# A transformer block on one core: first chunk of x on another DMA queue, the bias product one step later, seven warm-up products instead of nine

## The chip, the cores and the metric

The kernel runs on one core of a Trainium2 chip. The metric is the device time of one execution in microseconds (us). Before the change it is 303.93 us, the median of 3 runs (303.37 to 304.09). A run whose engines were recorded took 304.98 us, and its trace is what this document reads.

## The reference, cut to what matters

A single block on x of 256 tokens by 1024 columns, in float32. The part that stands at the start of the kernel is the input projection, and beside it a bias by distance for the attention's logits:

```
u    = rms_norm(x, mix_norm_g)              # x / rms(x) * g, row by row
proj = u @ w_in                             # 1024 -> 3*512 (q, k, v) + 2*512 (glu_a, glu_g)
attn = attention(q, k, v) with rel_bias[bucket(distance)] added to the logits, causal
conv = silu(layer_norm(depthwise_conv31(glu_a * sigmoid(glu_g))))
h    = x + concat(attn, conv) @ w_out
h    = h + (silu(un @ w_gate) * (un @ w_up)) @ w_down,   un = rms_norm(h, ffn_norm_g)
out  = rms_norm(h, final_norm_g)
```

## The kernel before, in words

All large products are made from float32 data split into two parts: a high part `wh` (or `uh`) and the rest `wl` (or `ul`), so each product is three: high by high, high by rest, rest by high. ScalarE (or VectorE for the first two pieces) makes the high part of a weight, and VectorE subtracts it for the rest. So every piece of a weight goes through a transfer (`raw_...`), a cast (`wh_...`) and a subtraction (`wl_...`) before TensorE has all three.

x lies transposed in `xs`, as 8 chunks (`k` = 0 to 7) of 128 columns by 256 tokens. `upper_u` (ScalarE) makes `uh[k]` from `xs[k]` and the gain in `pv`; `lower_u` (VectorE) makes `ul[k]`. The division by the root mean square of each token is not done there: it is applied to the products later, through `rb`, which comes from the sum of squares `accx`.

The first projection is worked in two halves. Step `a0.k` (function `a0`) does all for one chunk of the first half: cast, `uh`, `ul`, subtraction, and 12 matmuls of 128x256 into the banks `pa` and `pg` (`a_mm`). Steps `a1.i` do two chunks each of the second half with weights `a1_0` and `a1_1`. Between the steps of `a1` stand the sum of squares (`sq.k`, a square on ScalarE and an addition to `accx` on VectorE) and `rs` (`scale_x`), whose first instructions are TensorE's four small products `ps_x` with `accx`.

The order of all this is written out by hand, in the string `PROGRAM`: each word is a step, and every engine runs its own instructions in the order in which the steps issue them. `pz` (`bias_mm`) is the product of the table of the bias, `rbt`, with a constant one-hot matrix, `hot_s`; `zs` copies it out of the bank on ScalarE, `zd` sends it to memory from GpSimd's queue, and `bd` reads it back into `bias`, which `t.0` needs about 40 us into the run.

Transfers: SyncE's queue issues the pieces of the weights and the chunks of x in turn (lines 186 to 188). Of SyncE's and ScalarE's transfers at most eight are under way; a ninth waits for the landing of the one eight places before it. ScalarE's queue issues the first 28 columns of `pv`, which hold the gains (line 183). GpSimd's queue issues `hot_s` and `rbt` (lines 190 and 191), and after its fills the rest of `pv` (line 205). While the first data are on the way, TensorE runs `WARM` products of a matrix of ones with itself into a bank that nobody reads (line 194), which are there for its clock alone.

Of the kernel before, what the change touches and what calls it, by code (L numbers as in the profile page):

```python
# [16 lines left out]
S = 256  # L17
# [4 lines left out]
NB = 32  # L22
# [13 lines left out]
LOOK = 2  # L36
FINE = ("a0_0", "a0_4")
COPY_V = (("a0_0", 0), ("a0_0", 1))
WARM = 9

PROGRAM = """
ld.a1_0 a0.0 pz a0.1 a0.2 a0.3 zs zd ld.a1_1 a0.4 a0.5 a0.6 a0.7 ld.qk0
w.a1_0.0 sq.0 sq.1 w.a1_0.1 sq.2 sq.3 sq.4 ld.qk1 bd a1.0 w.a1_1.0 sq.5 sq.6 sq.7 h.a1_1.1 h.qk0.0 h.qk0.1 a1.1 rs
w.a1_1.1 w.qk0.0 ld.qk2 a1.2 rb glu.0 ud.0 w.qk0.1 ld.v0 us.0 a1.3 w.qk1.0 w.qk1.1 glu.1 ud.1 us.1 ld.qk3
qk.0.0 qk.0.1 qo.0 cw.0 h.qk2.0 h.qk2.1 qk.1.0 sc.0 qk.1.1 w.qk2.0 t.0 w.qk2.1 ct.0.0.1 ld.v1 qo.1 c.0.0 h.v0.0 n.0 ct.0.1.3 sc.1 t.1 h.v0.1 ct.0.3.4 w.v0.0
# [14 lines left out]
def block_kernel(ctx, tc, xT, w_in, w_out, w_gate, w_up, w_down, pvec, gfin, relb, hot, out):  # L60
# [10 lines left out]
    def mm(*args, **kw):  # L71
        return tc.keep_in_program_order(nc.tensor.matmul(*args, **kw))  # L72
# [12 lines left out]
    act, vec, pool, sync = (InOrder(e) for e in (nc.scalar, nc.vector, nc.gpsimd, nc.sync))  # L85

    def bank(i, name):
        return psum.tile([P, 512], F32, tag=f"b{i}", name=name)
# [78 lines left out]
    xs = const.tile([P, KD, S], F32, name="xs")  # L167
# [8 lines left out]
    rbt = w1.tile([NB + 1, H], F32, name="rbt")  # L176
    hot_s = w1.tile([NB + 1, ZN], F32, name="hot_s", tag="lg", bufs=2)
# [2 lines left out]
    wstk = [w1.tile([P, 8 * Q, 32], F32, name=f"wstk{i}", tag="wstk", bufs=2) for i in range(2)]  # L180
    invc = w1.tile([P, P], F32, name="invc")
    vec.memset(warm, 0.0)
    act.dma_start(pv[:, 0:PV_T], pvec[:, 0:PV_T])
    act.activation(warm, warm, AF.Sigmoid)
    first = [load(w_in, 2048 * i, f"a0_{4 * i}") for i in range(2)]
    for k in range(KD):
        next(first[k // 4])
        sync.dma_start(xs[:, k], xT[:, k * S : (k + 1) * S])
    pool.memset(ones, 1.0)
    pool.dma_start(hot_s, hot)  # L190
    pool.dma_start(rbt[0:NB, :], relb)
    wm = bank(4, "wm")
    for i in range(WARM):
        mm(wm[:, 0:P], ones, ones, start=i == 0, stop=i == WARM - 1)
    pool.memset(ident, 0.0)
    pool.affine_select(out=ident, in_=ident, compare_op=ALU.not_equal, fill=1.0, base=0,
                       pattern=[[-1, P]], channel_multiplier=1)
    pool.memset(mhalf, -0.5)
    pool.memset(rbt[NB : NB + 1, :], 1.0)
    for t in upad:  # L200
        pool.memset(t[:, 0 : TAPS - 1], 0.0)
        pool.memset(t[:, TAPS - 1 + S : UW + TAPS - 1], 0.0)
        pool.memset(t[:, UW + TAPS - 1 + S :], 0.0)
# [140 lines left out]
    zs = w1.tile([H, ZN], F32, name="zs", tag="lg", bufs=2)  # L344
    zd = dram.tile([H, ZN], F32, name="zd")
# [275 lines left out]
    for g in range(FG):  # L621
# [4 lines left out]
        if g == 0:  # L626
            act, vec, pool, sync = nc.scalar, nc.vector, nc.gpsimd, nc.sync
# [130 lines left out]
```

## Time and profile before

| | |
|---|---|
| median of the runs | 303.93 us (303.37 to 304.09) |
| the profiled execution | 304.98 us |
| its span, from the first to the last recorded instruction | 303.2 us |
| TensorE busy | 294.6 us, 97% of the span |
| VectorE, ScalarE, GpSimd busy | 72%, 55%, 3% |
| moved by the DMA engines | 56.39 MB, mean 186 GB/s over the span |

Reading it: the times in the trace are counted from the start of the span. PE is TensorE's matmul, DVE VectorE, ACT ScalarE, POOL GpSimd, SP SyncE; a q behind a name (SPq) is the part of the engine that issues transfers. A number in brackets behind a row is how long the engine had stood idle before it, and what released it. A float32 product shows as two matmul records, so the nine warm-up products are 18 records. All helpers that record an instruction have the line 72, 75 or 83, and the names in the rows tell them apart: `u` is `uh` and `ul`, and `raw_a`, `wh_a` and `wl_a` are the weights of both halves of the first projection.

### The profile page before, as it was taken

Reading aid. Unit: us, or ns where it says so; the run is one execution under the profiler, and the core shown is the slowest. Engines: PE = TensorE matmul, PEld = TensorE weight load, DVE = VectorE, ACT = ScalarE, POOL = GpSimd, SP = SyncE. Lnnn points to the kernel's source line nnn. Section 1 sums busy time; section 2 is a strip of 40 time slices with the busy share of each in tenths; the row PEclk is TensorE's granted clock in tenths of the full one; section 3 lists DMA queues with packets and bytes.
Section 4 is the critical chain, followed back from the end, with each engine's and each line's share of the span. In section 5 each row is a group of like instructions: output and inputs, shape, how many; then the busy total and the mean of one; then the engine's idle time right before and its main releaser. Section 6 shows DMA issues by size and latency. Waiting matters only on the chain.

```text
span 303.2 us, 5198 instructions
## 1 busy us (share of the span) xinstructions
PE 294.6 (97%) x1984; PEld 258.6 (85%) x1984; DVE 218.4 (72%) x405; ACT 166.6 (55%) x300; POOL 8.2 (3%) x27
## 2 busy tenths in 40 slices
PE   8999999999999999999999999999999999999991
PEld 8998987897699999878888888888888888888891
DVE  3877999888987788898665749485665748383483
ACT  3875554364583678674645636374645546371242
POOL 4000000000000000000000000000000000000000
PEclk9999999999999999999999999999999999999998
DMA  6999879744418426988583846648283837300012
GB/s 186 351 387 325 260 181 287 312 138 142 128 23 301 142 105 200 298 283 282 189 271 83 273 136 216 199 129 272 83 277 85 277 129 240 109 0 2 0 54 85
DMA packets 18936, 56.39 MB, mean 186 GB/s; under 512 B 2221, under 2 KB 5061, under 8 KB 18912
## 3 DMA queue, kind: packets, MB, share of 16 engines
q1 hardware_dynamic: 18176, 54.99, 56.4%
q0 software_dynamic: 304, 0.74, 0.9%
q8 instruction: 15, 0.25, 0.3%
q10 hardware_dynamic: 432, 0.34, 0.3%
q14 instruction: 9, 0.07, 0.1%
HBM read 54.41 MB, written 1.65 MB: 185 GB/s over the span
## 4 chain that ended last, share of the span: by engine, by line
PE 74%; issue 11%; DMA 6%; DVE 3%; ACT 3%; SPq 1%; POOL 1%; POOLq 0%; DVEq 0%
PE pf L72 34%; PE pd L72 17%; PE pqk L72 7%; DMA raw_a<-in_w_in 4%; PE pv L72 4%; PE pc L72 4%; PE py L72 2%; DMA raw_u<-in_w_up 2%; PE ps L72 1%; SPq L83 1%; ACT wh_a L83 1%; PE pa L72 1%; PE pg L72 1%; PE pt L75 1%; PE po L72 1%
## 5 line engine op out<-in xcount | busy, mean ns | idle before, releaser
L72 PE MATMUL pf<-u,wh_u 128*128 128x512 f32 (+1 forms) x192 | 64.1, 375 | 0.6 <-DVE ff L83 0.6
L72 PE MATMUL pf<-u,wh_g 128*128 128x512 f32 (+1 forms) x192 | 64.6, 377 | 0.0
L72 PE MATMUL pf<-u,wl_g 128*128 128x256 f32 x176 | 46.1, 281 | 0.0
L72 PE MATMUL pf<-u,wl_u 128*128 128x256 f32 x176 | 46.1, 281 | 0.0
L72 PEld LDWEIGHTS pf<-u,wh_u 128*128 128x128 f32 x192 | 34.9, 188 | 6.0 <-DVE ff L83 0.9
L72 PEld LDWEIGHTS pf<-u,wh_g 128*128 128x128 f32 x192 | 34.9, 188 | 5.3
L72 PEld LDWEIGHTS pf<-u,wl_u 128*128 128x128 f32 x176 | 33.1, 188 | 1.7
L72 PEld LDWEIGHTS pf<-u,wl_g 128*128 128x128 f32 x176 | 33.2, 188 | 1.5
L154 DVE TENSOR_TENSOR wl_u<-raw_u,wh_u 128x1024 fp32r<-128x1024 f32 x18 | 21.9, 1224 | 16.7 <-ACT wh_u L144 16.7
L72 PE MATMUL pd<-wh_d,fh 128*128 128x512 f32 (+1 forms) x88 | 33.7, 383 | 0.0
L72 PE MATMUL pd<-wh_d,fl 128*128 128x512 f32 (+1 forms) x88 | 33.5, 381 | 0.0
L72 PE MATMUL pd<-wl_d,fh 128*128 128x512 f32 (+1 forms) x88 | 33.4, 379 | 0.0
L144 ACT CAST wh_u<-raw_u 128x1024 fp32r<-128x1024 f32 x18 | 18.9, 1048 | 17.9 <-PE pd L72 9.6
L154 DVE TENSOR_TENSOR wl_d<-raw_d,wh_d 128x1024 fp32r<-128x1024 f32 x22 | 26.8, 1216 | 0.7 <-ACT wh_d L144 0.6
L154 DVE TENSOR_TENSOR wl_g<-raw_g,wh_g 128x1024 fp32r<-128x1024 f32 x18 | 22.0, 1223 | 4.7 <-ACT wh_g L144 4.3
L144 ACT CAST wh_g<-raw_g 128x1024 fp32r<-128x1024 f32 x18 | 18.9, 1050 | 9.0 <-PE pd L72 7.9
L144 ACT CAST wh_d<-raw_d 128x1024 fp32r<-128x1024 f32 x22 | 22.7, 1052 | 1.4 <-PE pd L72 1.1
L72 PE MATMUL pqk<-u,wh_qk 128*128 128x256 f32 x128 | 23.1, 282 | 0.0
L569 DVE TENSOR_TENSOR fb<-pf,fb 128x256 f32<-128x256 f32 x20 | 8.4, 419 | 19.1 <-ACT fb L568 19.1
L72 PEld LDWEIGHTS pqk<-u,wh_qk 128*128 128x128 f32 x128 | 19.6, 188 | 0.4 <-issue 0.3
L72 PEld LDWEIGHTS pd<-wh_d,fl 128*128 128x128 f32 x88 | 16.5, 188 | 3.5 <-DVE fl L585 0.2
L72 PEld LDWEIGHTS pd<-wl_d,fh 128*128 128x128 f32 x88 | 16.6, 188 | 3.3
(165 smaller groups left out, 580.7 us busy)
## 6 DMA issues: line engine op xcount, KB each, us to landing
raw_g<-in_w_gate SPq DMA_DIRECT2D x22, 512.0 KB, 4.5
raw_u<-in_w_up SPq DMA_DIRECT2D x22, 512.0 KB, 4.3
raw_d<-in_w_down SPq DMA_DIRECT2D x22, 512.0 KB, 4.7
raw_qk<-in_w_in SPq DMA_DIRECT2D x8, 512.0 KB, 7.1
raw_o<-in_w_out SPq DMA_DIRECT2D x8, 512.0 KB, 4.1
ustk<-ud SPq DMA_DIRECT2D x8, 288.0 KB, 5.7
raw_a<-in_w_in SPq DMA_DIRECT2D x8, 256.0 KB, 4.8
raw_a<-in_w_in SPq DMA_DIRECT2D x4, 512.0 KB, 7.4
```

Source lines behind the costliest of these rows:

```text
L72: return tc.keep_in_program_order(nc.tensor.matmul(*args, **kw))
L75: return tc.keep_in_program_order(nc.tensor.transpose(o, i, ident))
L83: return lambda *a, **k: tc.keep_in_program_order(f(*a, **k))
L144: act.copy(wh[:, c], raw[:, c])
L154: vec.tensor_sub(wl[:, c], raw[:, c], wh[:, c].bitcast(F32))
L569: vec.tensor_add(t, o[:, 0:S], t)
```

## The change

Three things are changed. The transfer of the first chunk of x leaves SyncE's queue and is issued first on ScalarE's, ahead of `pv`. The transfers of `hot_s` and `rbt` move on GpSimd's queue behind the fills of `ident`, `mhalf` and the last row of `rbt`, and their product `pz` moves from behind step `a0.0` to behind `a0.1`. `WARM` goes from 9 to 7.

```diff
-WARM = 9
+WARM = 7
-ld.a1_0 a0.0 pz a0.1 a0.2 a0.3 zs zd ld.a1_1 a0.4 a0.5 a0.6 a0.7 ld.qk0
+ld.a1_0 a0.0 a0.1 pz a0.2 a0.3 zs zd ld.a1_1 a0.4 a0.5 a0.6 a0.7 ld.qk0
     vec.memset(warm, 0.0)
+    act.dma_start(xs[:, 0], xT[:, 0:S])
     act.dma_start(pv[:, 0:PV_T], pvec[:, 0:PV_T])
     act.activation(warm, warm, AF.Sigmoid)
     first = [load(w_in, 2048 * i, f"a0_{4 * i}") for i in range(2)]
     for k in range(KD):
         next(first[k // 4])
-        sync.dma_start(xs[:, k], xT[:, k * S : (k + 1) * S])
+        if k > 0:
+            sync.dma_start(xs[:, k], xT[:, k * S : (k + 1) * S])
     pool.memset(ones, 1.0)
-    pool.dma_start(hot_s, hot)
-    pool.dma_start(rbt[0:NB, :], relb)
...
     pool.memset(mhalf, -0.5)
     pool.memset(rbt[NB : NB + 1, :], 1.0)
+    pool.dma_start(hot_s, hot)
+    pool.dma_start(rbt[0:NB, :], relb)
```

TensorE's first products before, from the warm-up on (`pa` and `pg` are the banks of the first half, `u2` holds `uh` and `ul`):

```order
L72 MATMUL wm_110<-ones_72 128x128 x9
L72 MATMUL pa0_137<-u2_70,wh_a0_0_0_154 128x256 x2
L72 MATMUL pg0_138<-u2_70,wh_a0_0_0_154 128x256 x2
L72 MATMUL pa0_137<-u2_70,wh_a0_0_0_154 128x256 x2
L72 MATMUL pg0_138<-u2_70,wh_a0_0_0_154 128x256 x2
L72 MATMUL pa0_137<-u2_70,wl_a0_0_0_155 128x256 x2
L72 MATMUL pg0_138<-u2_70,wl_a0_0_0_155 128x256 x2
L72 MATMUL pz_174<-hot_s_78,rbt_77 8x384
L72 MATMUL pa0_137<-u2_70,wh_a0_0_0_154 128x256 x2
```

Now, from the last two products of chunk 0 on (the number behind a bank's name is another in this build, the bank is the same):

```order
L72 MATMUL pa0_135<-u2_70,wl_a0_0_0_153 128x256 x2
L72 MATMUL pg0_136<-u2_70,wl_a0_0_0_153 128x256 x2
L72 MATMUL pa0_135<-u2_70,wh_a0_0_0_152 128x256 x2
L72 MATMUL pg0_136<-u2_70,wh_a0_0_0_152 128x256 x2
L72 MATMUL pa0_135<-u2_70,wh_a0_0_0_152 128x256 x2
L72 MATMUL pg0_136<-u2_70,wh_a0_0_0_152 128x256 x2
L72 MATMUL pa0_135<-u2_70,wl_a0_0_0_153 128x256 x2
L72 MATMUL pg0_136<-u2_70,wl_a0_0_0_153 128x256 x2
L72 MATMUL pz_188<-hot_s_78,rbt_77 8x384
L72 MATMUL pa0_135<-u2_70,wh_a0_0_1_154 128x256 x2
```

The product `pz` stood behind the 12 matmuls of chunk 0; it now stands behind the 24 of chunks 0 and 1.

GpSimd's instructions before, behind its first fills:

```order
L83 MEMSET ones 128x128
L83 DMA hot_s<-in_hot 33x384
L83 DMA rbt<-in_relb 32x8
L83 MEMSET ident 128x128
L83 ISA
L83 AFFINE_SELECT ident<-ident 128x128
L83 MEMSET mhalf 128x2
L83 MEMSET rbt 1x8
```

And the same place now:

```order
L83 MEMSET ones 128x128
L83 MEMSET ident 128x128
L83 ISA
L83 AFFINE_SELECT ident<-ident 128x128
L83 MEMSET mhalf 128x2
L83 MEMSET rbt 1x8
L83 DMA hot_s<-in_hot 33x384
L83 DMA rbt<-in_relb 32x8
```

The two transfers moved behind four short instructions; the fills of `upad` and `invc` and the transfer of the rest of `pv` follow them as they did.

SyncE's first transfers before (`raw_a0_0_0` and `raw_a0_0_1` hold the weights of chunks 0 and 1, and of 2 and 3):

```order
L83 DMA raw_a0_0_0_87<-in_w_in 128x512
L83 DMA xs_69<-in_xT 128x256
L83 DMA raw_a0_0_0_87<-in_w_in 128x512
L83 DMA xs_69<-in_xT 128x256
L83 DMA raw_a0_0_1_88<-in_w_in 128x512
L83 DMA xs_69<-in_xT 128x256
```

And now:

```order
L83 DMA raw_a0_0_0_88<-in_w_in 128x512 x2
L83 DMA xs_69<-in_xT 128x256
L83 DMA raw_a0_0_1_89<-in_w_in 128x512
L83 DMA xs_69<-in_xT 128x256
L83 DMA raw_a0_0_1_89<-in_w_in 128x512
```

The weights of chunk 1 and all behind them moved up by one transfer; the chunk of x that went from here is now the first instruction of ScalarE, ahead of `pv`.

## Rows read from the trace of the kernel before

**Rows 1.** The page: busy time and instructions of TensorE.

```profile
PE 294.6 (97%) x1984; PEld 258.6 (85%) x1984; DVE 218.4 (72%) x405; ACT 166.6 (55%) x300; POOL 8.2 (3%) x27
```

**Rows 2.** TensorE's waits, whole span: us in total, times, longest.

```profile
PE pf L72 <- DVE ff L83: 0.6, 1, 0.6
PE ps_x L72 <- DVE accx L83: 0.5, 1, 0.5
```

**Rows 3.** The chain that ended last, first 32 us: start, us, what.

```profile
4.49 5.85 DMA raw_a<-in_w_in
10.36 6.21 DMA raw_a<-in_w_in
```

**Rows 4.** The timeline up to TensorE's wait: start, us, engine, instruction.

```profile
16.60 1.05 ACT L83 CAST wh_a<-raw_a 128x1024 fp32r<-128x1024 f32 x1 [2.08 <-DMA raw_a<-in_w_in]
...
17.68 1.23 DVE L83 TENSOR_TENSOR wl_a<-raw_a,wh_a 128x1024 fp32r<-128x1024 f32 x1 [2.05 <-ACT wh_a L83]
...
23.55 0.39 PE L72 MATMUL pg<-u,wl_a 128*128 128x256 f32 x2
24.45 0.61 PE L72 MATMUL ps_x<-ones,accx 128*128 128x1 f32 x4 [0.51 <-DVE accx L83]
```

**Rows 5.** The timeline of TensorE, first 9 us.

```profile
1.00 4.21 PE L72 MATMUL wm<-ones 128*128 128x128 f32 x18 [1.00 <-POOL ones L83]
4.86 0.77 PE L72 MATMUL pa<-u,wh_a 128*128 128x256 f32 x2
...
6.29 0.59 PE L72 MATMUL pg<-u,wh_a 128*128 128x256 f32 x2
6.71 0.41 PE L72 MATMUL pa<-u,wl_a 128*128 128x256 f32 x2
6.96 0.39 PE L72 MATMUL pg<-u,wl_a 128*128 128x256 f32 x2
7.28 0.81 PE L72 MATMUL pz<-hot_s,rbt 33*8 33x384 f32 x2
8.02 0.50 PE L72 MATMUL pa<-u,wh_a 128*128 128x256 f32 x2
```

**Rows 6.** The timeline of the other engines and their queues, first 7 us.

```profile
0.74 0.41 ACTq L83 DMA_DIRECT2D pv<-in_pvec  x1
...
1.17 0.42 SPq L83 DMA_DIRECT2D xs<-in_xT  x1
...
1.29 0.70 POOL L83 DMA_DIRECT2D hot_s<-in_hot  x1 [0.35 <-issue]
...
2.51 0.22 POOL L83 MEMSET ident<- 128x128 f32 x1
...
3.21 0.10 POOL L83 MEMSET rbt<- 1x8 f32 x1
...
3.51 0.66 DVE L83 CAST wh_a<-raw_a 128x512 fp32r<-128x512 f32 x1 [2.63 <-DMA raw_a<-in_w_in]
...
3.97 0.51 ACT L83 ACTIVATE u<-xs,pv 128x256 fp32r<-128x256 f32 x1 [1.29 <-DMA xs<-in_xT]
...
6.93 0.51 ACT L83 ACTIVATE u<-xs,pv 128x256 fp32r<-128x256 f32 x1 [2.46 <-DMA xs<-in_xT]
```

**Rows 7.** Transfers of the first 30 us: KB each, median us to landing.

```profile
pv<-in_pvec POOLq DMA_DIRECT2D x1, 78.0 KB, 5.6
...
pv<-in_pvec ACTq DMA_DIRECT2D x1, 14.0 KB, 2.9
rbt<-in_relb POOLq DMA_DIRECT2D x1, 1.0 KB, 4.2
```

**Rows 8.** Stretches: busy per engine, granted clock, DMA share, GB/s.

```profile
4.00:5.00 1.00, 1.00 (x7) 1.00 (x6) 0.65 (x3) 0.48 (x1) 0.39 (x1) 1.00 0.54 158
5.00:6.00 1.00, 1.00 (x6) 1.00 (x6) 0.59 (x1) 0.00 (x0) 0.00 (x0) 1.00 0.77 219
6.00:8.00 2.00, 2.00 (x11) 1.24 (x9) 0.95 (x3) 0.51 (x2) 0.00 (x0) 1.00 1.00 330
```

## The prediction, made before the change was run

> **What bounds the kernel now.** I read the page first. TensorE is busy for 97% of the span [rows 1], so a change at the start counts only if TensorE's whole later work begins earlier or later. Next I read TensorE's waits over the whole span. There are three: the first microsecond before the warm-up, one of 0.5 us at `ps_x` for VectorE's `accx`, and one of 0.6 us at `pf` for VectorE [rows 2]. No wait of TensorE behind `ps_x` is for a transfer, so I take everything behind `ps_x` to follow it at a fixed distance. The question is then when `ps_x` starts, which is 24.45 us now.
>
> Two strands end there. TensorE itself arrives at 24.45 - 0.51 = 23.94 us. The other strand is the chain of waits, which runs back from `accx` to two transfers of `raw_a`, one after the other, from 4.49 to 16.60 us [rows 3]. ScalarE had stood idle for 2.08 us when the first piece of `a1_0` landed at 16.60, and VectorE for 2.05 us when that cast let it go on at 17.68 [rows 4]. So the later strand is a stream of transfers, and TensorE has 0.51 us to spare. The reader is to see that moving TensorE's start alone gives nothing: the stream must move too.
>
> The start itself comes from the timelines. The 18 warm-up records begin at 1.00 and the first real product at 4.86, which is (4.86 - 1.00) / 18 = 0.214 us a record [rows 5]. The first `uh` was ready at 3.97 + 0.51 = 4.48 [rows 6], so the warm-up holds TensorE for some 0.4 us too long. Chunk 1 comes late: its `uh` starts at 6.93 after an idle of 2.46 us for x [rows 6], and between 4 and 6 us the DMA engines moved only 158 and 219 GB/s, against 330 from 6 to 8 us [rows 8].
>
> **The clock.** The granted-clock column reads 1.00 in all these stretches [rows 8], but the spacing of the products contradicts it. Two products of 256 columns took 6.71 - 6.29 = 0.42 us, so 0.21 each, which is 256 columns at 1.2 GHz. From 6.71 the next two took 0.25 [rows 5], and from 8.02 to 23.55 there are 130 products (7 chunks of the first half and 4 of the second, 12 each, less the last two), 0.119 each [rows 4, 5], the level of 2.4 GHz. TensorE had been busy without a break from 1.00 to 6.71 when the clock rose.
>
> **The change part by part.**
>
> Fewer warm-ups: 14 records of 0.214 us end at 4.00 instead of 4.84. What is late next is the first chunk. Its x went out at 1.17 and `uh` started at 3.97, 2.80 us later [rows 6]. Issued at 0.74, the same 2.80 give 3.54. But now `pv` is behind it on the same queue: one issue of some 0.43 us later, at 1.17, and with its 2.9 us to landing [rows 7] at 4.07. So `uh` starts at about 4.07 and ends at 4.58; TensorE begins at about 4.6. At best `pv` is not delayed and x decides: 3.54 + 0.51 = 4.05. At worst the weights of chunk 0 are held up by the 128 KB of x beside them: at 158 GB/s that is 0.8 us, so the cast starts at 3.51 + 0.8, takes 0.66, and the start is 5.0. I take 4.6, since both transfers are nearest to their own rows.
>
> TensorE's early work: from 4.6 to 6.71 it does 2.1 / 0.214 = 10 of the 12 products of chunk 0, and the other two at 0.119 end at 6.95. Chunk 1 then takes 12 x 0.119 = 1.43 to 8.38, `pz` its 8.02 - 7.28 = 0.74 to 9.12. Before, chunk 1 ended at 8.02 + 1.43 = 9.45 with `pz` ahead of it. The gain is 0.33 us, if chunk 1 is there: its x moves up one issue of 0.42 [rows 6], so `uh` would end at 6.93 - 0.42 + 0.51 = 7.02, as good as in time. If chunk 1 comes no earlier, TensorE waits until 7.44 for it and the gain turns to a loss of 0.16. Either is covered by the 0.51 us.
>
> `pz` later: moved on GpSimd's queue past `ident` to the fill of `rbt`, 3.31 - 2.51 = 0.80 us of work [rows 6], the two transfers go out 0.45 to 0.80 us later (the idle of 0.35 before the first may be gone). `rbt` follows `hot_s` by 0.70 and lands at latest at 1.29 + 0.80 + 0.70 + 4.2 = 7.0; with the 5.6 us of the longest transfer of that queue it is 8.4 [rows 6, 7]. `pz` wants it at 8.38, so no wait. Behind `pz` on TensorE stands chunk 2, and ScalarE's copy `zs` behind it is wanted some 30 us before the bias is used: nothing.
>
> The stream: SyncE has one issue of 0.42 us less, but its later transfers wait for earlier landings, and all bytes still pass by the time `a1_0` lands. What can move the landing at 16.60 is the slack stretch from 4 to 6 us. If `hot_s` and `rbt` cause it and, sent later, no longer do, then (330 - 158) + (330 - 219) = 283 KB come back, at 330 GB/s 0.86 us [rows 8]. If they cause it wherever they stand, nothing comes back; and if it falls into a full stretch for the 0.8 us by which they are moved, that costs 0.8 x (330 - 219) / 330 = 0.27 us. So between -0.27 and +0.86. I take a gain of 0.2, near the middle but on the low side, because the two transfers are moved by less than 0.8 us and the slack lasts for two.
>
> Sum: `ps_x` starts at the later of 23.94 - 0.33 = 23.61 and 24.45 - 0.2 = 24.25. That is 0.2 us earlier. The profiled execution (304.98, of which 303.2 is the span) would give 304.8; it lay 1.05 above the median, and I take the same 0.2 off the median: 303.7 us.
>
> **The rivals.**
>
> The slack in the stream goes away with the move. The stream would allow 0.86, TensorE's arrival then decides: 24.45 - 23.61 = 0.84 us, so 303.1. For it: the slack stands exactly where `hot_s` and `rbt` are on the way (issued at 1.29, landing 4.2 later). Against it: they still go out ahead of chunk 1's landing.
>
> Nothing comes of it: the stream of weights lands as before, `ps_x` stays, 303.9. For it: the bytes are the same. The Trainium skill (DMA: Bandwidth & Descriptors, section "Issuing engines are not separate DMA queues") says that transfers of all issuing engines run on the same 16 DMA engines, and that another issuer saves only the time on the sequencer. By that rule x's new queue is worth one issue and the stream nothing, and this rival would be the forecast; the row of the issue, 0.42 us, agrees as to its size, and no row here shows two such queues carrying large transfers.
>
> It is slower: the clock rises later. The warm-up now ends at 4.00, TensorE stands for 0.6 us, and then runs in small pieces if chunk 1 is late. If the unbroken run that came ahead of the rise, 1.00 to 6.71, must be made anew from 4.6, the rise comes at 10.3, 3.6 us later. In these TensorE does at 0.214 what it did at 0.119 and loses 3.6 x (1 - 0.119 / 0.214) = 1.6 us; it arrives at 23.61 + 1.6 = 25.2, 0.75 after the present start: 304.7. It decides from a loss above 24.45 - 23.61 = 0.84, that is a rise put off by 1.9 us. Against it: the gap is a tenth of that run, and what is needed for the rise no row shows. The skill (TensorE: Matmul & The Clock Gate, "Part 1: The HAM clock gate") says that the default state is the throttled one and that activity releases it. That agrees with the rise at 6.71; it does not tell what 0.6 us cost here.
>
> **How the numbers follow.** 0.48 for the forecast, 0.17 for the slack gone (303.1), 0.20 for nothing (303.9), 0.15 for the late clock (304.7). The runs of one kernel lie 0.7 us apart, so a difference below 0.3%, 0.9 us (from 303.0 to 304.8), cannot be told from none. Of the first rival half falls below 303.0, of the last half above 304.8, and some scatter is added at both ends: faster 0.13, the same 0.76, slower 0.11. The range of 302.9 to 304.7 takes in the first rival and most of the last.
>
> **What would show it.** In the profile after: TensorE's first real product at 4.2 to 5.0; the rise of the clock, by the spacing of the products, at about 6.7; `pz` behind chunk 1 without a wait; the first cast of `a1_0` at 16.4 instead of 16.60; `ps_x` at 24.25, still waiting for `accx`. The forecast is wrong if TensorE's list has a new wait for a transfer, if the spacing is still 0.21 at 8 us, or if `ps_x` moves by more than 0.5 us either way.

## The result, and the profile after

The changed kernel takes 305.98 us (median of 22 runs, 303.77 to 307.47), the kernel before beside it 304.08 us (22 runs, 303.37 to 306.18). The ratio is 1.0053, with an interval of 1.0036 to 1.0070: slower by half a per cent, some 1.6 us (the medians differ by 1.9), where 0.2 us less was forecast. The runs after fall into two groups: 4 lie between 303.8 and 304.6, 18 between 305.7 and 307.5. Of the 22 before one lies above 305.6.

The profiled execution after took 305.9 us, its span is 304.1. TensorE's waits, whole span (us in total, times, longest):

```profile
PE pa L72 <- ACT u L83: 1.9, 1, 1.9
PE wm L72 <- POOL ones L83: 1.0, 1, 1.0
PE pf L72 <- DVE ff L83: 0.2, 1, 0.2
```

The wait at `ps_x` is gone and a longer one has come, at the first real product; the wait at `pf` fell from 0.6 us to 0.2 [rows 2]. The chain of waits now starts with `pv` instead of the weights [rows 3]:

```profile
0.74 0.41 ACTq L83
1.18 4.46 DMA pv<-in_pvec
5.73 0.52 ACT u L83
6.29 0.50 PE pa L72 x2
```

The reader is to see that the last thing chunk 0 waited for is the 14 KB of `pv`, 4.46 us under way. It went out at 1.18, as forecast, behind the first chunk of x. Before, with nothing ahead of it on its queue, it took 2.9 [rows 7]. The landing times of ScalarE's queue after (KB each, median us to landing):

```profile
xs<-in_xT ACTq DMA_DIRECT2D x1, 128.0 KB, 4.0
...
pv<-in_pvec ACTq DMA_DIRECT2D x1, 14.0 KB, 4.5
```

The chunk of x takes 4.0 us here, and its `uh` had started 2.80 us after its issue when SyncE sent it [rows 6]. The weights of chunk 0 are late too. VectorE's and ScalarE's first work, of the timeline after:

```profile
4.59 0.43 DVE L83 CAST wh_a<-raw_a 128x512 fp32r<-128x512 f32 x1 [3.72 <-DMA raw_a<-in_w_in]
...
5.73 0.94 ACT L83 ACTIVATE u<-xs,pv 128x256 fp32r<-128x256 f32 x2 [2.57 <-DMA pv<-in_pvec]
...
15.91 1.04 ACT L83 CAST wh_a<-raw_a 128x1024 fp32r<-128x1024 f32 x1
```

The cast of chunk 0 starts at 4.59 instead of 3.51, the first `uh` at 5.73 instead of 3.97 [rows 6]. The last row of the three says that the stream of weights did come forward: the first piece of `a1_0` was cast at 15.91, with no wait for it, where it was waited for until 16.60 [rows 4]. It did not help, because TensorE was later still. TensorE's start after:

```profile
1.00 3.36 PE L72 MATMUL wm<-ones 128*128 128x128 f32 x14 [1.00 <-POOL ones L83]
6.29 0.50 PE L72 MATMUL pa<-u,wh_a 128*128 128x256 f32 x2 [1.94 <-ACT u L83]
...
6.86 0.45 PE L72 MATMUL pa<-u,wh_a 128*128 128x256 f32 x2
...
8.14 0.63 PE L72 MATMUL pa<-u,wh_a 128*128 128x256 f32 x2
8.57 0.63 PE L72 MATMUL pg<-u,wh_a 128*128 128x256 f32 x2
8.99 0.63 PE L72 MATMUL pa<-u,wh_a 128*128 128x256 f32 x2
...
10.83 0.97 PE L72 MATMUL pz<-hot_s,rbt 33*8 33x384 f32 x2
11.73 0.50 PE L72 MATMUL pa<-u,wh_a 128*128 128x256 f32 x2
...
25.84 0.50 PE L72 MATMUL ps_x<-ones,accx 128*128 128x1 f32 x4
```

TensorE stands for 1.94 us and then runs chunk 0 at the full clock: 12 products from 6.29 to 8.14. Chunk 1 then takes 0.43 us for two products (8.14, 8.57, 8.99), the level of 1.2 GHz. The clock had risen, and it fell back. The stretches (busy per engine, granted clock, DMA share, GB/s) say the same:

```profile
6.00:8.00 2.00, 1.71 (x12) 1.64 (x13) 1.73 (x4) 1.62 (x4) 0.00 (x0) 0.94 1.10 386
8.00:12.00 4.00, 4.00 (x18) 2.97 (x18) 2.69 (x6) 1.32 (x4) 0.00 (x0) 0.60 1.05 358
12.00:16.00 4.00, 4.00 (x36) 4.00 (x36) 2.73 (x6) 4.00 (x10) 0.52 (x1) 1.00 0.98 367
```

TensorE got 0.60 of its clock from 8 to 12 us and did 18 matmul records there, against 36 in the next four. The sum of the trace: chunk 2 starts at 11.73, and before it started at 9.54, by this row of the timeline before:

```profile
9.54 0.40 PE L72 MATMUL pa<-u,wh_a 128*128 128x256 f32 x2
```

These 2.19 us are 1.43 for the late first product (6.29 against 4.86), -0.57 for chunk 0 (1.85 against 2.42 us, since it met the full clock), 1.17 for chunk 1 (2.69 against 1.52) and 0.16 for `pz` (0.90 against 0.74). The 0.51 us that TensorE had to spare, and somewhat shorter spacing behind, leave 1.39 us at `ps_x` (25.84 against 24.45); the shorter wait at `pf` gives back 0.4, and the span is 0.9 longer.

### The profile page after: what moved, and what is told of

Read it like the earlier page. It is cut to its first block, busy times and chain, and to the rows that moved or that the text cites. A ratio compares the mean times of both kernels' runs of the same rounds, so it can differ in the third digit from the quotient of the medians.

```text
span 304.1 us, 5189 instructions
## 1 busy us (share of the span) xinstructions
PE 294.4 (97%) x1980; PEld 258.0 (85%) x1980; DVE 217.6 (72%) x405; ACT 166.4 (55%) x300; POOL 8.1 (3%) x27
## 4 chain that ended last, share of the span: by engine, by line
PE 80%; issue 11%; DMA 3%; DVE 2%; ACT 1%; POOL 1%; POOLq 0%; ACTq 0%; DVEq 0%
PE pf L72 34%; PE pd L72 17%; PE pqk L72 7%; PE pa L72 4%; PE pg L72 4%; PE pv L72 4%; PE pc L72 4%; PE py L72 2%; DMA raw_u<-in_w_up 1%; DMA pv<-in_pvec 1%; PE ps L72 1%; PE pt L75 1%; PE po L72 1%; DVE ht L650 1%; PE ph L75 1%
```

## The experiments

Ten kernels, timed beside the kernel before. Ratios are to the kernel before of the same series, with 95% intervals. "Gap" is TensorE's idle time between the warm-up and the first real product in the profiled execution. First each part of the change alone.

**The first chunk of x alone.**

```diff
+    act.dma_start(xs[:, 0], xT[:, 0:S])
     act.dma_start(pv[:, 0:PV_T], pvec[:, 0:PV_T])
...
-        sync.dma_start(xs[:, k], xT[:, k * S : (k + 1) * S])
+        if k > 0:
+            sync.dma_start(xs[:, k], xT[:, k * S : (k + 1) * S])
```

> The kernel before with one part of the change: the first chunk of x leads ScalarE's queue, ahead of pv; nine warm-ups and the bias inputs stand as before. Theory 1 (the late first chunk is the cause: x and pv on the second queue share the DMA engines with the weights of chunks 0 and 1, and pv lands behind x): pv lands about 4.5 us after its issue as in the changed kernel, the first real product starts at 5.8 to 6.4 us instead of 4.86, TensorE stands for 1.0 to 1.5 us behind the warm-up; the time is 305 to 306 us. Theory 2 (the two warm-ups fewer are the cause): the warm-up is whole, so 303.7 to 304.3 us. Theory 3 (the later bias product is the cause, by ScalarE's wait for it): 303.7 to 304.3 us.

Measured: ratio 1.0016 (0.9987 to 1.0046), median 304.73 us, 3 of 12 runs at 306.1 to 307.4. Its timeline:

```profile
6.37 0.50 PE L72 MATMUL pa<-u,wh_a 128*128 128x256 f32 x2 [1.16 <-ACT u L83]
...
24.54 0.50 PE L72 MATMUL ps_x<-ones,accx 128*128 128x1 f32 x4
```

The data are as late as in the changed kernel (`pv` 4.5 us to landing, first product at 6.37), yet `ps_x` starts at 24.54, and the time is not clear of no change. Theory 1 as I put it falls here: the lateness is right, but it is covered in most runs. The median lies above what theories 2 and 3 allowed as well (304.3), so this run alone decides nothing between them (the kernel before itself came to 304.38 in this series, with 5 of 35 runs above 305.6).

**The bias inputs and their product alone.**

```diff
-    pool.dma_start(hot_s, hot)
-    pool.dma_start(rbt[0:NB, :], relb)
...
     pool.memset(rbt[NB : NB + 1, :], 1.0)
+    pool.dma_start(hot_s, hot)
+    pool.dma_start(rbt[0:NB, :], relb)
...
-ld.a1_0 a0.0 pz a0.1
+ld.a1_0 a0.0 a0.1 pz
```

> The kernel before with one part of the change: the two bias inputs are sent later and their product stands behind chunk 1; x, pv and the nine warm-ups stand as before. Theory 1 (the late first chunk is the cause): no loss; the slack of the DMA engines between 4 and 6 us is smaller, the first piece of a1_0 lands up to 0.8 us before 16.60, and ps_x moves forward by up to 0.8 us: 303.2 to 304.0 us. Theory 2 (fewer warm-ups): the same. Theory 3 (the later bias product makes ScalarE wait): 305 to 306 us, with an idle of 2 us or more on ScalarE before the copy out of pz.

Measured: 1.0003 (0.9981 to 1.0024), 304.80 us. `ps_x` starts at 24.08 and the first piece of `a1_0` is cast at 15.29. ScalarE has no wait before the copy of `pz`. Theory 3 falls. The gain that theories 1 and 2 expected (303.2 to 304.0) did not come either: the profiled execution, at 304.13 the shortest of the 12, is not typical of them.

**Two warm-ups fewer alone** (`WARM = 7`).

> The kernel before with one part of the change: seven warm-ups instead of nine. Theory 1 (the late first chunk is the cause): the first product starts at about 4.55 us, 0.55 us behind the end of the warm-up; no loss beyond 0.3 us: 303.8 to 304.4 us. Theory 2 (the two warm-ups fewer are the cause, through the clock): the clock falls back or rises 2 us or more later, 305 to 306 us. Theory 3: 304 us.

Measured: 0.9979 (0.9955 to 1.0004), 303.81 us; the first product starts at 4.51 behind a gap of 0.16 us. Theory 2 falls in its simple form: fewer warm-ups cost nothing that could be measured as long as the data come at 4.5 us. The profiled execution is the longest of the 12, 306.0 us. It has no late stretch of half-rate products: its first piece of `a1_0` is cast only at 17.20, `ps_x` starts at 25.05, and the span behind that is 0.4 us longer than before. So a run above 305.6 us does not by itself tell of the clock.

**The changed kernel with 14 warm-ups** (`WARM = 14`), so that the data are late but TensorE is not idle.

> The changed kernel with 14 warm-ups, so that TensorE has no gap before the first real product. The start of that product stays at 6 to 6.6 us (or 7.0, if the warm-up runs to its end at the lower clock). Theory 1 in its first form (the late data cost their lateness alone, 1.4 us): 305.3 us or more. Theory 1 in its second form (the lateness is covered, and the loss is the clock that falls back after the gap of 1.9 us): no stretch of products at 0.21 us behind the rise, ps_x at 24.0 to 24.6 us, 303.7 to 304.4 us. Theory 3 (the later bias product): 305 to 306 us.

Measured: 0.9997 (0.9976 to 1.0019), 304.67 us, no run of 12 above 305.6. Its timeline:

```profile
1.00 5.83 PE L72 MATMUL wm<-ones 128*128 128x128 f32 x28 [1.00 <-POOL ones L83]
6.58 0.48 PE L72 MATMUL pa<-u,wh_a 128*128 128x256 f32 x2
...
8.07 0.40 PE L72 MATMUL pa<-u,wh_a 128*128 128x256 f32 x2
...
24.41 0.50 PE L72 MATMUL ps_x<-ones,accx 128*128 128x1 f32 x4
```

This settles the main point. The first product is even later than in the changed kernel (6.58 against 6.29), everything else is the same, and seven products of ones more, which nobody reads, take the loss away: `ps_x` starts at 24.41 instead of 25.84. So the loss is not the wait for data as such, within the interval of 0.2% either way; it is the clock.

**The gap alone:** the kernel before with `WARM = 3`, no transfer touched.

> The kernel before with three warm-ups instead of nine, nothing else: the transfers are those of before, so chunk 0 is ready at about 4.5 us, and the warm-up ends at 1.00 + 6 x 0.214 = 2.3 us. TensorE stands for some 2.2 us, as long as in the changed kernel, without late data. Theory A (the gap between the warm-up and the first product costs, through TensorE's clock): the clock rises only after 7.5 us or falls back once, the median is 305 to 306.5 us and the runs fall into two groups. Theory B (late data of chunk 0 are needed for the loss): no more than 304.6 us.

Measured: 1.0073 (1.0050 to 1.0096), 306.57 us, 8 of 9 runs above 305.6. Its timeline:

```profile
4.66 0.79 PE L72 MATMUL pa<-u,wh_a 128*128 128x256 f32 x2 [2.01 <-ACT u L83]
5.25 0.63 PE L72 MATMUL pg<-u,wh_a 128*128 128x256 f32 x2
...
11.61 0.63 PE L72 MATMUL pa<-u,wh_a 128*128 128x256 f32 x2
12.04 0.63 PE L72 MATMUL pg<-u,wh_a 128*128 128x256 f32 x2
...
14.07 0.40 PE L72 MATMUL pa<-u,wh_a 128*128 128x256 f32 x2
14.31 0.40 PE L72 MATMUL pg<-u,wh_a 128*128 128x256 f32 x2
...
26.67 0.50 PE L72 MATMUL ps_x<-ones,accx 128*128 128x1 f32 x4
```

Here the first product is on time (4.66) and the loss is larger than the change's: in this execution two products take 0.42 us or more from the first on and 0.24 only from 14 us on. The clock did not fall back here, it rose late. Theory B, that late data are needed, falls: three warm-ups and a gap of two microseconds ahead of the real work are enough. Whether the gap does it or the six products that are missing from the warm-up, this run does not tell; two fewer, with a gap of 0.16, cost nothing measurable.

**The changed kernel with `pv` ahead of x** on ScalarE's queue.

```diff
-    act.dma_start(xs[:, 0], xT[:, 0:S])
     act.dma_start(pv[:, 0:PV_T], pvec[:, 0:PV_T])
+    act.dma_start(xs[:, 0], xT[:, 0:S])
```

> The changed kernel with the two transfers of ScalarE's queue in the other order: pv first, then the first chunk of x. Theory A1 (the place behind x makes pv late, and pv alone holds chunk 0): pv lands at about 3.7, x at 4.6 to 5.2 us, the first product starts at 5.0 to 5.8 instead of 6.29, the gap is 1.0 to 1.6 us and the time falls to 304.3 to 305.3 us. Theory A2 (the second queue as such is slow, whatever its order, since it shares the DMA engines with the weights of chunks 0 and 1): the first product stays at 5.9 us or later and the time at 305.3 us or more.

Measured: 1.0034 (1.0013 to 1.0055), 305.49 us. `pv` is back to 3.0 us to landing, x takes 3.9:

```profile
xs<-in_xT ACTq DMA_DIRECT2D x1, 128.0 KB, 3.9
...
pv<-in_pvec ACTq DMA_DIRECT2D x1, 14.0 KB, 3.0
```

Its other rows:

```profile
3.61 0.53 DVE L83 CAST wh_a<-raw_a 128x512 fp32r<-128x512 f32 x1 [2.74 <-DMA raw_a<-in_w_in]
...
5.77 0.80 PE L72 MATMUL pa<-u,wh_a 128*128 128x256 f32 x2 [1.42 <-ACT u L83]
6.37 0.63 PE L72 MATMUL pg<-u,wh_a 128*128 128x256 f32 x2
...
9.32 0.40 PE L72 MATMUL pa<-u,wh_a 128*128 128x256 f32 x2
9.55 0.40 PE L72 MATMUL pg<-u,wh_a 128*128 128x256 f32 x2
```

The first product starts at 5.77, the gap is 1.42 us, and the order of the two costs 0.5 us of the lateness. So both theories have a part: A1 for the start, and A2 for the rest, since x is still slower there than behind the weights on SyncE's queue. The start and the gap lie in A1's ranges, the time in A2's (305.3 or more). The weights of chunk 0 are nearly on time again: their cast starts at 3.61. And the clock rose late here too: two products take 0.42 us or more from the first on and 0.23 only from 9.32.

**The changed kernel with nine warm-ups** (`WARM = 9`).

> The changed kernel with the nine warm-ups of before. The warm-up ends at 4.85, chunk 0 is ready at 5.8 to 6.3, so the gap is 1.0 to 1.4 us instead of 1.9. Theory A (the gap costs through the clock, and its length decides how often): between the changed kernel and the one with 14 warm-ups, 304.5 to 305.3 us, most runs near 304.6 and some above 306. Theory C (any gap of a microsecond costs the same as one of two): 305.5 us or more.

Measured: 1.0026 (1.0003 to 1.0049), 305.06 us, a gap of 1.49 us; 5 of 12 runs above 305.6, the others at 304.3 to 305.3. It lies between the changed kernel and the one with 14 warm-ups, as theory A has it, but its interval overlaps both of theirs. The profiled execution has all its real products at the full rate and `ps_x` at 24.33, so no trace shows what the five runs paid.

**The changed kernel with x back on SyncE's queue.**

```diff
-    act.dma_start(xs[:, 0], xT[:, 0:S])
...
-        if k > 0:
-            sync.dma_start(xs[:, k], xT[:, k * S : (k + 1) * S])
+        sync.dma_start(xs[:, k], xT[:, k * S : (k + 1) * S])
```

> The changed kernel with one part undone: the first chunk of x goes out from SyncE's queue as before; seven warm-ups and the late bias inputs and product stay. Theory A (the gap, made by the late first chunk, costs through the clock): the first product starts at 4.5 to 4.8 us, the gap is 0.2 to 0.8 us and the loss of 0.5% is gone: 303.7 to 304.7 us. Rival (the other two parts of the change together cost, though neither did alone): 305.3 us or more.

Measured: 1.0023 (1.0011 to 1.0035), 304.77 us (the kernel before 303.91), no run of 12 above 305.3. The upper group of runs is gone, but some 0.7 us of loss stay: the time lies just above theory A's range (up to 304.7), and what the rival says, that the other two parts together cost, holds for this rest, though not at its size (305.3 or more). TensorE's rows:

```profile
4.63 0.50 PE L72 MATMUL pa<-u,wh_a 128*128 128x256 f32 x2 [0.28 <-ACT u L83]
...
7.82 0.50 PE L72 MATMUL pa<-u,wh_a 128*128 128x256 f32 x2 [1.32 <-ACT u L83]
...
9.61 0.81 PE L72 MATMUL pz<-hot_s,rbt 33*8 33x384 f32 x2
```

Chunk 1 comes no earlier (its `uh` starts at 7.26, before at 6.93), so TensorE waits 1.32 us for it, where `pz` used to fill 0.74 us of that time [rows 5]; `pz` then costs its own time behind. That would be this rest, but it is argued from one trace, in which `ps_x` starts at 24.58, hardly later than before. All products behind the wait of 1.32 us ran at the full rate here: a gap of that length, behind chunk 0, did not bring the clock down.

**Two versions that might have beaten both**: x on SyncE's queue and nine warm-ups as before, the bias inputs sent late, their product behind chunk 0; and the same with two more products of ones behind it.

```diff
+        for i in range(2):
+            mm(wm[:, 0:P], ones, ones, start=i == 0, stop=i == 1)
```

> A version that may beat both: the kernel before, where only the two transfers of the bias inputs are sent later on GpSimd's queue; their product keeps its place behind chunk 0, where TensorE stood for 0.5 us in the kernel with the late product. If the transfers land by 7.2 us as they did there (issued at 1.6 to 2.3, 3.9 and 4.4 us to landing), TensorE fills that wait, ps_x starts at 23.6 to 24.1 us, and the time is 303.2 to 304.0 us. If they land later, TensorE waits for them and the time stays at 304.2 to 304.8 us.

> A version that may beat both: the bias inputs sent late, their product behind chunk 0, x and the nine warm-ups as before, and two more products of ones behind the bias product, which fill TensorE's wait of 0.4 us for chunk 1. If the runs above 305.6 us of the kernel without the filling come from the clock after small gaps, they get fewer and the median falls to 303.3 to 304.0 us. If not, 304.2 to 304.8 us.

Measured: 1.0010 (0.9985 to 1.0036), 304.62 us, and 1.0016 (1.0001 to 1.0032), 304.61 us. The profiled executions show what was hoped for: `ps_x` starts at 23.47 and 23.77, and the first has a span of 301.3. The medians do not follow, so neither expectation of a gain held and no version beats the kernel before. In the first the clock had risen within the warm-up (18 records in 3.86 us, before 4.21). One execution with a lucky clock is not a result.

## Why the prediction was wrong

In order of the gap, the runs read: 14 warm-ups, no gap, 0.9997; x alone, 1.16 us, 1.0016; `pv` first, 1.42, 1.0034; nine warm-ups, 1.49, 1.0026; the change, 1.94, 1.0053; three warm-ups, 2.01, 1.0073. (Their intervals overlap from one to the next; the ends are clear.) Seven warm-ups alone fit the row, 0.16 and 0.9979; x back on SyncE's queue does not, 0.28 and 1.0023. The number of warm-ups differs as well along this row, so how much is the gap and how much the length of the warm-up is not shown.

**What bounds the kernel.** Right: everything behind `ps_x` follows it. From `ps_x` to the end of the span it is 303.2 - 24.45 = 278.7 us before, 304.1 - 25.84 = 278.3 after, and 278.2 in the kernel with three warm-ups. The 0.4 us between are the wait at `pf`. Of the other nine traces seven give 277.8 to 278.5; the two at 279.2 (seven warm-ups alone, and the changed kernel with nine) have a further wait, at `pc` for VectorE, of 0.3 and 0.7 us.

**The first chunk, the step that failed.** "I take 4.6, since both transfers are nearest to their own rows", within 4.2 and 5.0. It was 6.29. The mis-sized term is the landing of `pv`: I took 2.9 us from a row where its queue was empty, and behind 128 KB of x it is 4.5. I had bounded the weights' delay by what x takes beside them, 0.8 us (it was 1.08, 4.59 against 3.51), and for `pv` I had added only the issue. The weights, for their part, were slower with x issued at the same 0.74 us on a second queue (cast at 4.59) than with x behind them on their own (3.51); with x on the second queue behind `pv` they were not (3.61). The Trainium skill (DMA: Bandwidth & Descriptors, section "Issuing engines are not separate DMA queues") says that all queues run on the same 16 engines and another issuer saves only sequencer time. The trace agrees for the first chunk: 4.0 us to landing for x there, and nothing of chunk 0 came earlier for having two queues.

**The gap.** It was forecast at 0.6 us and came out at 1.94 by the trace's end of the warm-up (2.3 from the 4.00 of the forecast), because the warm-up was cut by two products for data that came later, not earlier. This would be why neither part alone shows the loss: x alone leaves a gap of 1.16, fewer warm-ups alone 0.16, and together they make 1.94; that the loss goes with this length is argued from the row above.

**The clock.** The rival that came true was named, with a chance of 0.15. Its course was another in the profiled execution: I let the rise come later, and there the clock rose and fell back once, for a stretch with 0.60 of it between 8 and 12 us. With `pv` first and with three warm-ups the course was the rival's: no product at the full rate before 9 and 13.7 us. Its price, 1.6 us at the lower clock, less what TensorE has to spare, was 304.7; the late first product was not in it. The Trainium skill (TensorE: Matmul & The Clock Gate, "Part 1: The HAM clock gate") makes the throttled state the default and has activity release it. The traces agree in that each begins at the lower level and reaches the full one only after some work. They show nothing so simple for the moment: in the changed kernel the 14 records of the warm-up took 3.36 us, the same as with `pv` first, where the next products still ran at the lower level; yet its first real products, at 6.29, ran at the full one, so the rise seems to have come while TensorE stood. Which execution pays no trace here foretells, and that the runs of the changed kernel fall into two groups suggests that it changes from one execution to the next; only one of each kernel has a trace.

**The bias product and the stream.** No wait for `rbt` came, as forecast. ScalarE waited 2.6 us for `pz` in the changed kernel (not foreseen), and it cost nothing: TensorE has no wait between its first real product and `ps_x`. The stream came forward by more than the 0.2 us forecast: 15.91 or sooner instead of 16.60, and 15.32 and 15.29 with x or the bias inputs moved alone. Identical transfers gave 16.54 and 17.20 in two other executions (three and seven warm-ups), so a trace by itself is good to some 0.7 us. Still, all four traces with the bias inputs late and x in its place have the cast at 15.04 to 15.72, so either part seems to bring it forward, by about a microsecond; the four with both have it at 15.68 to 16.08. The reason was not the forecast one. The slack between 4 and 5 us was filled when x moved and `hot_s` and `rbt` stayed (x alone, first row), and it stood when they moved and x stayed (x back on SyncE's queue, second row):

```profile
4.00:5.00 1.00, 1.00 (x6) 0.91 (x5) 0.27 (x1) 0.00 (x0) 0.39 (x1) 1.00 0.98 264
4.00:5.00 1.00, 0.72 (x5) 0.42 (x5) 0.52 (x2) 0.51 (x1) 0.00 (x0) 1.00 0.46 140
```

So the two small transfers did not cause it (158 GB/s before [rows 8]), and what brings the stream forward when they move stays open. In the changed kernel it was of no use, since TensorE was the later of the two.

## What to carry to other kernels

Filler work ahead of the first data is to last until the data are there: too much of it costs what it holds up, nothing measurable with 14 products here, and too little cost up to 0.7% here, by a clock that fell back or rose late. Size it from the measured start of the first real product after the change, never together with a change that is meant to bring the data sooner. When a transfer is put ahead of another on a queue, the second's landing must be taken behind the first one's bytes, however small it is itself.

## What the runs showed that I had not expected

The granted-clock column reads 1.00 from the first microsecond, also where two products of 256 columns take 0.43 us (up to 6.7 us before, up to 13.7 with three warm-ups); only the spacing of the products shows the lower level there.

The moment of the rise changes a good deal between executions. With nine warm-ups and no long wait behind them, two products still take 0.42 us up to 6.7 us in the kernel before; in the kernel with the bias inputs late and their product behind chunk 1 they take 0.24 from 5.85 on, and in the one with that product behind chunk 0 they take 0.34 or less from the first, at 4.74.

A transfer of 14 KB took 2.9 to 3.1 us to land with its queue empty and 4.5 behind one of 128 KB, in all four kernels that had it there.
